# Up product of the second MLP with both halves of the normalised activation in one 512-column operand, from the sixth block on

## The chip, the cores and the metric

One core of a Trainium2 chip runs the whole kernel. The metric is the device time of one execution in microseconds, as the median of several runs; the profile is of one further execution of the same program.

## The reference, cut to what matters

Two decoder layers over 256 tokens of width 1024. Each ends in a gated MLP with a short causal convolution, and the change is in the second of these two MLPs:

```python
def rms_norm(x, gain):
    y = xf * lax.rsqrt(jnp.mean(xf * xf, axis=-1, keepdims=True) + NORM_EPS)
    return (y * gain)

def conv_ffn(x, gain, w_up, conv_w, conv_b, w_down):
    h = rms_norm(x, gain)
    up = causal_dwconv(h @ w_up, conv_w, conv_b)      # 3 taps along the tokens
    g, v = up[..., :D_FF], up[..., D_FF:]             # D_FF = 2816
    return (jax.nn.silu(g) * v) @ w_down
```

All inputs and outputs are float32.

## The kernel before, in words

**Products in three parts.** A float32 product is made of three float32r matmuls: each operand is split into a rounded part (hi) and the rest (lo), and hi·hi, hi·lo and lo·hi are added up in PSUM. `mm3` (L259 to L262) issues the three; L260 and L261 use the weights' hi part with the activation's hi and lo part, L262 the weights' lo part with the activation's hi part. In the up product the weight block is the stationary operand and 256 tokens are the moving columns, so every matmul there has 256 columns and loads its own weights.

**Weights.** `Stream` (L82 to L132) brings every weight tile from HBM over SyncE's queue (L98), and splits it: ScalarE writes the hi part `whi` (L115), VectorE the lo part `wlo` (L119), both of 128x1024. `get` keeps four tiles split ahead; five buffers rotate for each of the two parts, three for the raw tile.

**The MLP** (`ffn`, L508). `split_x` (L341, L342) multiplies x by the norm's gain and splits it; the factor 1/rms per token, `rb`, is not in this operand. The 22 blocks f of 128 hidden channels then follow: 48 matmuls each (2 halves j, gate and value, by 8 chunks k of the width, by 3) into one PSUM bank of 512 columns, gate in the left half and value in the right half (tile `psU`). Banks come from two pools of two, `br` and `bw`, block by block in turn, so four blocks can be in flight. `post` (L524) then takes the bank: L526 multiplies by `rb` from PSUM to SBUF (128x512, VectorE), L531 (ScalarE) and L533 (VectorE) are the convolution, L537 to L539 the gate, L542 and L543 split the result into `ah` and `al`. From the sixth block on (`LAG = 5`), after the up matmuls of block f come the 12 down matmuls of block f-5 (L562; 512 columns each, tile `acc`); after the last block, the down product of the remaining blocks follows.

**Order.** In this part no order is written out by hand. The tile framework plans the order of each engine's queue when the program is built, from its own estimates of durations and from how soon each result is needed; the trace shows the order that it chose. Only in the first layer is a part of the order written by hand. The final norm begins after the last down matmuls.

Of the kernel before, what the change touches and what calls it, by code (L numbers as in the profile page):

```python
# [10 lines left out]
F32 = mybir.dt.float32  # L11
F32R = mybir.dt.float32r
BF16 = mybir.dt.bfloat16
I32 = mybir.dt.int32
AF = mybir.ActivationFunctionType
ALU = mybir.AluOpType
# [3 lines left out]
T = 256  # L20
KT = D // 128
# [5 lines left out]
FT = FF // 128  # L27
# [6 lines left out]
RAW_AHEAD = 2  # L34
SPLIT_AHEAD = 4
LAG = 5
NR = 8


# [100 lines left out]
def _body(ctx, tc, a):  # L140
    nc = tc.nc
    V, S, G, PE, L = nc.vector, nc.scalar, nc.gpsimd, nc.tensor, nc.sync
# [6 lines left out]
    def slots(pool, tag, bufs):  # L149
        return lambda shape, dt=F32, name="t": pool.tile(shape, dt, name=name, tag=tag, bufs=bufs)  # L150

    def banks(pool, tag, bufs):
        return lambda name="ps": pool.tile([128, 512], F32, name=name, tag=tag, bufs=bufs)
# [4 lines left out]
    ba, br, bw = banks(pp, "acc", 4), banks(pp, "r", 2), banks(pp, "w", 2)  # L158
# [25 lines left out]
    def ffn_order(l):  # L184
# [3 lines left out]
        for f in range(FT):  # L188
            o += [up(f), up(FT + f)]
            if LAG <= f < FT - 4 + LAG:  # L190
                o.append(dn(f - LAG))
        o += [dn(f) for f in range(FT - LAG, FT - 4)]
        if l:
# [5 lines left out]
    def by_steps(steps, **lists):  # L199
# [18 lines left out]
    W = Stream(nc, order, rawp, hlp, lambda key: [gains[:, 2 + key[1], 2 * key[2] + i:2 * key[2] + i + 1]  # L218
                                                  for i in range(2)] if key[0] == "mkv" else [None])
# [3 lines left out]
    def views(pool, name, *shapes):  # L223

        n = [int(np.prod(s_)) for s_ in shapes]
        t = pool.tile([128, sum(n)], F32, name=name)
        out = []
        for i, s_ in enumerate(shapes):
            ax = " ".join(f"a{j}" for j in range(len(s_)))
            v = t[:, sum(n[:i]):sum(n[:i + 1])]  # L230
            out.append(v.rearrange(f"p ({ax}) -> p {ax}", **{f"a{j}": d for j, d in enumerate(s_)}))
        return out

    x, gains, ident, s5p, rtok, ones, nhalf, convp, maskf, ropeC, ropeS, rbm, vm1 = views(
        const, "held", (KT, T), (8, KT), (128,), (3, NP), (2,), (1,), (1,), (2, 4, 2 * FT), (128,), (T,), (T,), (T,),
        (2, MEMW))
# [22 lines left out]
    def mm3(out, whi, wlo, ahi, alo, first, last):  # L259
        PE.matmul(out, whi, ahi, start=first, stop=False, skip_group_check=True)  # L260
        PE.matmul(out, whi, alo, start=False, stop=False, skip_group_check=True)  # L261
        PE.matmul(out, wlo, ahi, start=False, stop=last, skip_group_check=True)  # L262
# [8 lines left out]
    def squares(src, ts=None):  # L271
        ts = [] if ts is None else ts
        for s_ in src:
            t = sq([128, 512], name="sq")
            S.activation(t, s_, AF.Square)  # L275
            ts.append(t)
        return ts
# [12 lines left out]
    def root(p):  # L290

        m = sm.tile([128, 2], F32, name="m")
        V.tensor_scalar(m, p[:, :2], 1.0 / D, EPS, op0=ALU.mult, op1=ALU.add)
        return newton(m, 2)
# [21 lines left out]
    def rms(src, bk=bw):  # L316
        y = root(sums(squares(src), bk))
        rb = sm.tile([128, T], F32, name="rb", bufs=2)
        S.activation(rb, spread(y, bk), AF.Copy)
        return rb, y  # L320

    def xbanks():
        return [x[:, 2 * b:2 * b + 2].rearrange("p a t -> p (a t)") for b in range(4)]

    def rb2(rb):
        return rb[:, None, :].to_broadcast([128, 2, T])

    def v2(ap):
        return ap.rearrange("p (a t) -> p a t", t=T)
# [178 lines left out]
    def ffn(l, gi):  # L508
        with tc.tile_pool(name=f"ffn{l}", bufs=1) as pool:
            sl, sa = slots(pool, "s", 12), slots(pool, "a", 2 * LAG + 2)  # L510
            act = split_x(gi)
            rb, _ = rms(xbanks(), bk=bw if l else ba)
            dacc = None
            if l:

                dacc = [ba("acc") for _ in range(4)]
                for k in range(KT):
                    for t in range(2):
                        c = 128 * (k % 4)
                        PE.matmul(dacc[2 * t + k // 4][:, c:c + 128], x[:, k, 128 * t:128 * t + 128], ident,  # L520
                                  start=k % 4 == 0, stop=False, skip_group_check=True)
            acts = {}

            def post(f, p):  # L524
                u = sl([128, 2, T], name="u")
                V.tensor_mul(u, v2(p), rb2(rb))  # L526
                y = sl([128, 2, T], name="y")
                for j in range(2):
                    c = j * FT + f
                    cp = lambda i: convp[:, l, i, c:c + 1]  # L530
                    S.activation(y[:, j], u[:, j], AF.Identity, bias=cp(3), scale=cp(2))  # L531
                    for d in (1, 2):
                        V.scalar_tensor_tensor(y[:, j, d:], u[:, j, :T - d], cp(2 - d), y[:, j, d:],  # L533
                                               op0=ALU.mult, op1=ALU.add)
                g, v = y[:, 0], y[:, 1]
                th = sl([128, T], name="th")
                S.activation(th, g, AF.Tanh, scale=0.5)  # L537
                V.scalar_tensor_tensor(th, th, 1.0, g, op0=ALU.add, op1=ALU.mult)
                V.tensor_mul(th, th, v)  # L539
                ah, al = sa([128, T], F32R, "ah"), sa([128, T], F32R, "al")  # L540
                if l:
                    S.activation(ah, th, AF.Copy, scale=0.5)  # L542
                    V.scalar_tensor_tensor(al, th, 0.5, ah.bitcast(F32), op0=ALU.mult, op1=ALU.subtract)  # L543
                else:
                    S.activation(ah, th, AF.Copy)
                    V.tensor_sub(al, th, ah.bitcast(F32))
                acts[f] = (ah, al)

            def down(f):
                if l:  # L550
                    whi, wlo = W.get(("dn", l, f))
                    for t in range(2):
                        down_tokens(t, (0, 1), f, whi, wlo, False)
                else:
                    gemm(dacc, ("dn", l, f), (f,), acts.get, 0, 8, f == 0, False)

            def down_tokens(t, hs, f, whi, wlo, last):

                ah, al = (p[:, 128 * t:128 * t + 128] for p in acts[f])
                for a_, w_ in ((ah, whi), (ah, wlo), (al, whi)):  # L560
                    for i, h in enumerate(hs):
                        PE.matmul(dacc[2 * t + h], a_, w_[:, 512 * i:512 * i + 512], start=False,  # L562
                                  stop=last and a_ is al, skip_group_check=True)

            for f in range(FT):
                p = (br if f % 2 else bw)("psU")
                w = [None, None]
                todo = [(j, k) for j in range(2) for k in range(KT)]
                for j, k in todo:
                    if w[j] is None:  # L570
                        w[j] = W.get(("up", l, j * FT + f))
                    c = slice(128 * k, 128 * k + 128)
                    mm3(p[:, 256 * j:256 * j + 256], w[j][0][:, c], w[j][1][:, c], *act(k),
                        k == 0 and j == 0, k == KT - 1)
                post(f, p)
                if LAG <= f < FT - 4 + LAG:
                    dacc = dacc or [ba("acc") for _ in range(4)]
                    down(f - LAG)
            for f in range(FT - LAG, FT - 4):
                down(f)  # L580
            if l:
                for h in range(2):
                    for ks in (LAST[:2], LAST[2:]):
                        whi, wlo = W.get(("dnq", l, ks, h))
                        for t in range(2):
                            for i, f in enumerate(ks):
                                c = slice(512 * i, 512 * i + 512)
                                down_tokens(t, (h,), f, whi[:, c], wlo[:, c], f == FT - 1)
                return dacc
            for b in range(4):  # L590
                gemm(dacc, ("dnq", l, b), LAST, acts.get, 2 * b, 2, False, True)
            residual(dacc, 0.5)


    def layer0(pool, s5):
        sr, sh = slots(pool, "r", NR), slots(pool, "h", 4)
        sc = [slots(pool, f"c{i}", 4 - 3 * i) for i in range(2)]
# [617 lines left out]
    with tc.tile_pool(name="fin", bufs=1) as pool:  # L1215
# [4 lines left out]
        for t in range(2):  # L1220
# [7 lines left out]
            for h in range(2):  # L1228
                o = so([128, 512], name="o")
                V.scalar_tensor_tensor(o, accs[2 * t + h], y, gf[h], op0=ALU.mult,  # L1230
                                       op1=ALU.mult)
# [52 lines left out]
```

## Time and profile before

| | |
|---|---|
| median of 3 runs | 671.42 us (670.06 to 672.51) |
| profiled execution | 671.97 us |
| its span, first to last instruction | 670.2 us (1.77 us lie around it) |
| TensorE (PE) busy | 629.2 us, 94% |
| VectorE (DVE) busy | 547.5 us, 82% |
| ScalarE (ACT) busy | 408.0 us, 61% |
| GpSimd (POOL) busy | 103.7 us, 15% |
| second MLP, first up matmul to last down matmul | 472.4 to 662.4 us |

All times of the trace are microseconds from the start of the span. Durations of matmuls overlap (a new one starts every 0.12 or 0.23 us while each takes 0.28 or 0.39 us by the profile), so what one costs is read from the distance of the starts. VectorE's records overlap a little as well: a 128x256 operation of 0.42 us is followed by the next after 0.34 us.

### The profile page before, as it was taken

The numbers are of one execution on the slowest core, as the hardware profiler recorded it, in microseconds if no ns is written. First come the engines' busy times: TensorE is split into PE (matmuls) and PEld (weight loads), VectorE is DVE, ScalarE is ACT, GpSimd is POOL, SyncE is SP. The second block draws the span as 40 slices with busy tenths as digits, with TensorE's granted clock in tenths as the row PEclk, the third lists the DMA queues.
The fourth block names the chain that finished last, engine by engine and source line by source line (L and its number), as shares of the span: only waits on it lengthen the run. The fifth ranks groups of instructions, "written<-read, shape, count | busy, mean of one in ns | idle before, by whom it ended". The sixth has DMA issues, their size and how long they took to land.

```text
span 670.2 us, 12678 instructions
## 1 busy us (share of the span) xinstructions
PE 629.2 (94%) x4968; PEld 595.2 (89%) x4968; DVE 547.5 (82%) x1011; ACT 408.0 (61%) x746; POOL 103.7 (15%) x117
## 2 busy tenths in 40 slices
PE   6787597999999999999999998999999999999995
PEld 5676586899999999999999997879999999999984
DVE  7989899786699988787769799875479998888872
ACT  5597454675566556565548788774446665555641
POOL 4596303031200000000003226301200000000000
PEclk9799698899999999999999997999999999999998
DMA  8722313256457436455465142424345555555511
GB/s 301 253 96 63 104 48 119 95 190 220 155 191 251 169 117 236 157 205 188 149 237 173 65 166 99 150 73 165 109 138 189 193 183 186 186 188 189 189 33 63
DMA packets 43356, 105.24 MB, mean 157 GB/s; under 512 B 3744, under 2 KB 14240, under 8 KB 43296
## 3 DMA queue, kind: packets, MB, share of 16 engines
q1 hardware_dynamic: 42720, 103.84, 45.6%
q8 instruction: 39, 0.64, 0.4%
q10 hardware_dynamic: 576, 0.59, 0.3%
q14 instruction: 21, 0.17, 0.1%
HBM read 103.37 MB, written 1.05 MB: 156 GB/s over the span
## 4 chain that ended last, share of the span: by engine, by line
PE 76%; DVE 18%; ACT 2%; issue 2%; DMA 0%; POOL 0%; DVEq 0%; ACTq 0%
PE psU L262 13%; PE psU L260 12%; PE psU L261 12%; PE acc L562 9%; PE acc L261 7%; PE acc L262 7%; PE acc L260 7%; DVE wlo L119 2%; DVE X L642 1%; PE psO L481 1%; DVE xt L642 1%; PE ps L388 1%; DVE cf L649 1%; DVE Vd L642 1%; PE psT L465 1%
## 5 line engine op out<-in xcount | busy, mean ns | idle before, releaser
L115 ACT ACTIVATE whi<-wraw 128x1024 fp32r<-128x1024 f32 (+1 forms) x176 | 181.1, 1037 | 102.7 <-PE psU L261 52.0
L119 DVE TENSOR_TENSOR wlo<-wraw,whi 128x1024 fp32r<-128x1024 f32 (+1 forms) x176 | 212.8, 1212 | 31.2 <-PE psU L262 14.9
L262 PE MATMUL psU<-xhi,wlo 128*128 128x256 f32 x704 | 197.6, 281 | 1.1 <-DVE wlo L119 1.1
L260 PE MATMUL psU<-xhi,whi 128*128 128x256 f32 x704 | 198.0, 282 | 0.0
L261 PE MATMUL psU<-xlo,whi 128*128 128x256 f32 x704 | 197.4, 281 | 0.0
L262 PEld LDWEIGHTS psU<-xhi,wlo 128*128 128x128 f32 x704 | 133.2, 189 | 1.4 <-DVE wlo L119 1.3
L261 PEld LDWEIGHTS psU<-xlo,whi 128*128 128x128 f32 x704 | 132.6, 189 | 0.7
L260 PEld LDWEIGHTS psU<-xhi,whi 128*128 128x128 f32 x704 | 132.4, 188 | 0.7
L533 DVE SCALAR_TENSOR_TENSOR y<-u,held,y 128x254 f32<-128x254 f32 (+1 forms) x176 | 77.9, 477 | 1.5 <-ACT y L531 1.3
L531 ACT ACTIVATE y<-u,held 128x256 f32<-128x256 f32 x88 | 47.7, 590 | 20.6 <-DVE u L526 20.6
L526 DVE TENSOR_TENSOR u<-psU,rb 128x512 f32<-128x512 f32 x44 | 30.3, 688 | 33.3 <-PE psU L262 33.1
L261 PE MATMUL acc<-al,whi 128*128 128x256 f32 x176 | 49.6, 282 | 0.0
L260 PE MATMUL acc<-ah,whi 128*128 128x256 f32 x176 | 49.6, 282 | 0.0
L262 PE MATMUL acc<-ah,wlo 128*128 128x256 f32 x176 | 49.6, 282 | 0.0
L280 POOL TENSOR_TENSOR sq<-sq 128x512 f32<-128x512 f32 x5 | 8.2, 1648 | 229.7 <-ACT sq L275 229.7
L866 PE MATMUL acc<-xg,wraw 128*128 128x256 f32 x128 | 34.5, 431 | 5.5 <-ACT xg L856 5.5
L866 PEld LDWEIGHTS acc<-xg,wraw 128*128 128x128 f32 x128 | 27.8, 222 | 10.0 <-ACT xg L856 5.5
L262 PEld LDWEIGHTS acc<-ah,wlo 128*128 128x128 f32 x176 | 33.6, 191 | 0.0
L261 PEld LDWEIGHTS acc<-al,whi 128*128 128x128 f32 x176 | 33.6, 191 | 0.0
L260 PEld LDWEIGHTS acc<-ah,whi 128*128 128x128 f32 x176 | 33.5, 190 | 0.0
L262 PE MATMUL acc<-xhi,wlo 128*128 128x256 f32 x112 | 31.6, 283 | 0.0
L261 PE MATMUL acc<-xlo,whi 128*128 128x256 f32 x112 | 31.4, 281 | 0.0
(253 smaller groups left out, 1322.8 us busy)
## 6 DMA issues: line engine op xcount, KB each, us to landing
wraw<-w_up SPq DMA_DIRECT2D x88, 512.0 KB, 4.2
wraw<-w_down SPq DMA_DIRECT2D x44, 512.0 KB, 4.0
wraw<-w_out SPq DMA_DIRECT2D x16, 512.0 KB, 3.6
wraw<-w_in SPq DMA_DIRECT2D x15, 512.0 KB, 5.7
wraw<-w_mem_kv SPq DMA_DIRECT2D x8, 512.0 KB, 3.8
wraw<-w_kv SPq DMA_DIRECT2D x6, 512.0 KB, 7.4
wraw<-w_kv SPq DMA_DIRECT2D x8, 384.0 KB, 3.4
wraw<-w_glu SPq DMA_DIRECT2D x6, 384.0 KB, 3.7
```

Of the source, the lines that this page charges most:

```text
L115: self.nc.scalar.activation(hi[:, c], t[:, c], AF.Copy, scale=1.0 if g_ is None else g_)
L119: self.nc.vector.tensor_sub(lo[:, c], t[:, c], hi[:, c].bitcast(F32))
L260: PE.matmul(out, whi, ahi, start=first, stop=False, skip_group_check=True)
L261: PE.matmul(out, whi, alo, start=False, stop=False, skip_group_check=True)
L262: PE.matmul(out, wlo, ahi, start=False, stop=last, skip_group_check=True)
L280: G.tensor_add(ts[0], ts[0], ts[1])
L526: V.tensor_mul(u, v2(p), rb2(rb))
L531: S.activation(y[:, j], u[:, j], AF.Identity, bias=cp(3), scale=cp(2))
L533: V.scalar_tensor_tensor(y[:, j, d:], u[:, j, :T - d], cp(2 - d), y[:, j, d:], op0=ALU.mult, op1=ALU.add)
L562: PE.matmul(dacc[2 * t + h], a_, w_[:, 512 * i:512 * i + 512], start=False, stop=last and a_ is al, skip_group_check=True)
L642: V.tensor_tensor(o, a_, b_, op=op)
L866: PE.matmul(acc[2 * h + b][:, 256 * (m % 2):256 * (m % 2) + 256], w[:, 512 * i + 128 * m:512 * i + 128 * m + 128], xg[k // 2][:, k % 2], s ...
```

## The change

In the second MLP, from block 5 on (`NORMED = (FT, 5)`: never in the first MLP), the activation operand is the fully normalised x. `normalise(b)`, called in blocks 1 to 4 for two chunks of the width each, multiplies x by gain and by `rb` on VectorE (into `xn`), takes the hi part on ScalarE and the lo part on VectorE, and leaves both side by side in one tile `hl[k]` of 2x256 columns. The up product of these blocks then has two matmuls for each half and chunk: weights' hi part with all 512 columns (hi and lo), and weights' lo part with the 256 hi columns. Each half has a PSUM bank of its own, one of `br` and one of `bw`, with the main sum left and the hi·lo sum right; `post` copies the right half to SBUF on ScalarE and adds the left one to it on VectorE, in place of the product with `rb`. Two new tags take SBUF: 8 tiles `n` and 2 tiles `g` of 2 KB a partition.

```diff
+NORMED = (FT, 5)
...
+            sn, sg, hl = slots(pool, "n", KT * l), slots(pool, "g", 2 * l), []
...
+            def normalise(b):
+
+                t = sg([128, 2, T], name="xn")
+                for i in range(2):
+                    k = 2 * b + i
+                    V.scalar_tensor_tensor(t[:, i], x[:, k], gains[:, gi, k:k + 1], rb, op0=ALU.mult, op1=ALU.mult)
+                for i in range(2):
+                    n = sn([128, 2, T], F32R, "xhl")
+                    S.activation(n[:, 0], t[:, i], AF.Copy)
+                    V.tensor_sub(n[:, 1], t[:, i], n[:, 0].bitcast(F32))
+                    hl.append(n)
+
             def post(f, p):
                 u = sl([128, 2, T], name="u")
-                V.tensor_mul(u, v2(p), rb2(rb))
+                if f < NORMED[l]:
+                    V.tensor_mul(u, v2(p), rb2(rb))
+                else:
+                    for j in range(2):
+                        S.activation(u[:, j], p[j][:, T:], AF.Copy)
+                        V.tensor_add(u[:, j], p[j][:, :T], u[:, j])
...
             for f in range(FT):
-                p = (br if f % 2 else bw)("psU")
-                w = [None, None]
-                todo = [(j, k) for j in range(2) for k in range(KT)]
-                for j, k in todo:
-                    if w[j] is None:
-                        w[j] = W.get(("up", l, j * FT + f))
-                    c = slice(128 * k, 128 * k + 128)
-                    mm3(p[:, 256 * j:256 * j + 256], w[j][0][:, c], w[j][1][:, c], *act(k),
-                        k == 0 and j == 0, k == KT - 1)
+                p = (br if f % 2 else bw)("psU") if f < NORMED[l] else [b_("psU") for b_ in (br, bw)]
+                for j in range(2):
+                    whi, wlo = W.get(("up", l, j * FT + f))
+                    for k in range(KT):
+                        c = slice(128 * k, 128 * k + 128)
+                        if f < NORMED[l]:
+                            mm3(p[:, 256 * j:256 * j + 256], whi[:, c], wlo[:, c], *act(k), k == 0 and j == 0, k == KT - 1)
+                        else:
+                            PE.matmul(p[j], whi[:, c], hl[k].rearrange("p a t -> p (a t)"), start=k == 0, stop=False,
+                                      skip_group_check=True)
+                            PE.matmul(p[j][:, :T], wlo[:, c], hl[k][:, 0], start=False, stop=k == KT - 1,
+                                      skip_group_check=True)
+                if l and 0 < f <= 4:
+                    normalise(f - 1)
                 post(f, p)
```

## Rows read from the trace of the kernel before

**Rows 1.** The page: busy time by engine, and the clock in 40 slices.

```profile
PE 629.2 (94%) x4968; PEld 595.2 (89%) x4968; DVE 547.5 (82%) x1011; ACT 408.0 (61%) x746; POOL 103.7 (15%) x117
...
PEclk9799698899999999999999997999999999999998
```

**Rows 2.** The chain that ended last, from 470 us on, by line.

```profile
by line: PE acc L562 29.7%; PE psU L262 20.9%; PE psU L260 20.9%; PE psU L261 20.7%; PE acc L520 1.8%; DVE o L1230 0.8%; DVE wlo L119 0.6%; issue 0.5%; PE ps L286 0.4%; ACT sq L1223 0.3%; DVEq L1280 0.3%; POOL y L299 0.3%; PE ps L312 0.2%; 
```

**Rows 3.** Busy time in three stretches: PE, PEld, DVE, ACT, POOL, clock, DMA, GB/s.

```profile
485.31:490.69 5.38, 5.38 (x48) 5.38 (x47) 1.23 (x2) 1.08 (x2) 0.00 (x0) 1.00 0.45 157
490.69:513.15 22.46, 22.46 (x181) 21.92 (x179) 21.77 (x38) 14.90 (x24) 0.00 (x0) 1.00 0.48 161
513.15:646.22 133.07, 133.07 (x950) 125.07 (x948) 113.59 (x186) 79.37 (x117) 0.00 (x0) 1.00 0.55 178
```

**Rows 4.** TensorE in order of time, blocks 5 to 21: start, duration, instruction.

```profile
510.35 0.63 PE L562 MATMUL acc<-whi,ah 128*128 128x512 f32 x2
...
513.15 0.28 PE L260 MATMUL psU<-xhi,whi 128*128 128x256 f32 x1
...
515.97 0.28 PE L260 MATMUL psU<-xhi,whi 128*128 128x256 f32 x1
...
518.84 0.63 PE L562 MATMUL acc<-whi,ah 128*128 128x512 f32 x2
...
527.30 0.62 PE L562 MATMUL acc<-whi,ah 128*128 128x512 f32 x2
...
530.09 0.28 PE L260 MATMUL psU<-xhi,whi 128*128 128x256 f32 x1
...
646.22 0.62 PE L562 MATMUL acc<-whi,ah 128*128 128x512 f32 x2
```

**Rows 5.** TensorE in order of time, last 48 down matmuls: first and last.

```profile
651.77 0.39 PE L562 MATMUL acc<-whi,ah 128*128 128x512 f32 x1
...
662.42 0.39 PE L562 MATMUL acc<-whi,al 128*128 128x512 f32 x1
```

**Rows 6.** Groups by line and shape, from 450 us: busy us, mean ns.

```profile
L526 DVE TENSOR_TENSOR u<-psU,rb 128x512 f32<-128x512 f32 x22 | 15.1, 688 | 15.0 <-PE psU L262 15.0
L539 DVE TENSOR_TENSOR th<-th,y 128x256 f32<-128x256 f32 x22 | 9.3, 421 | 0.4
L543 DVE SCALAR_TENSOR_TENSOR al<-th,ah 128x256 fp32r<-128x256 f32 x22 | 9.2, 420 | 1.8 <-ACT ah L542 1.5
L542 ACT ACTIVATE ah<-th 128x256 fp32r<-128x256 f32 x22 | 9.0, 408 | 4.1 <-DVE th L539 4.1
L342 DVE SCALAR_TENSOR_TENSOR xlo<-held,xhi 128x256 fp32r<-128x256 f32 x8 | 4.5, 606 | 0.0
L504 DVE TENSOR_TENSOR olo<-psO,ohi 128x256 fp32r<-128x256 f32 x2 | 0.8, 424 | 5.0 <-ACT ohi L503 5.0
L319 ACT ACTIVATE rb<-ps 128x256 f32<-128x256 f32 x1 | 0.4, 385 | 9.1 <-PE ps L312 9.1
```

**Rows 7.** VectorE in order of time: the bank evacuations, and the last block's end.

```profile
490.69 0.69 DVE L526 TENSOR_TENSOR u<-psU,rb 128x512 f32<-128x512 f32 x1 [1.66 <-PE psU L262]
...
517.94 0.68 DVE L526 TENSOR_TENSOR u<-psU,rb 128x512 f32<-128x512 f32 x1
518.54 0.41 DVE L543 SCALAR_TENSOR_TENSOR al<-th,ah 128x256 fp32r<-128x256 f32 x1
...
544.50 0.69 DVE L526 TENSOR_TENSOR u<-psU,rb 128x512 f32<-128x512 f32 x1 [0.54 <-PE psU L262]
...
652.47 0.43 DVE L543 SCALAR_TENSOR_TENSOR al<-th,ah 128x256 fp32r<-128x256 f32 x1 [0.48 <-ACT ah L542]
```

**Rows 8.** Waits from 490 to 655 us: us in total, times, longest.

```profile
ACT whi L115 <- PE psU L261: 30.7, 27, 2.4
...
DVE wlo L119 <- PE psU L262: 2.3, 4, 1.0
```

**Rows 9.** TensorE in order of time: its one wait in the second MLP.

```profile
481.54 0.39 PE L262 MATMUL psU<-xhi,wlo 128*128 128x256 f32 x1 [1.14 <-DVE wlo L119]
```

## The prediction

> **What bounds the kernel now.** The page comes first: TensorE is busy for 94% of the span and its clock is full nearly everywhere [rows 1]. Next is the chain that ended last, from 470 us on, because the change lies there: 62.5% of it are the three up matmuls and 29.7% the down matmuls [rows 2], so the second MLP ends when TensorE has worked through its stream. The table by stretches says how near the others are. From 485 to 646 us TensorE is busy without a gap at clock 1.00. VectorE has 4.15 us free of 5.38 just after the norm's factor is there, then almost nothing (21.77 busy of 22.46 us, blocks 2 to 5), then some room (113.59 of 133.07 us); ScalarE has room all along and GpSimd does nothing [rows 3]. So a microsecond less on TensorE is a microsecond less of time, as long as VectorE, the tight one in blocks 0 to 5, does not come to stand in its way.
>
> **What it removes on TensorE.** Blocks 5 to 21 are 17 blocks of 16 pairs (half, chunk), 272 pairs. In each, two 256-column matmuls on the same weights become one of 512 columns; the third one stays. What one costs is the distance of the starts. From the first down matmul of block 5 (510.35) to that of block 21 (646.22) are 16 blocks in 135.87 us, 8.492 us a block; 12 of its matmuls are down matmuls of 512 columns, which took 2.79 us in the block shown (527.30 to 530.09), 0.2325 us each [rows 4]. The 48 up matmuls thus take 8.492 - 2.79 = 5.70 us, 0.1188 us each. A second price of 512 columns is in the tail: 48 matmuls from 651.77 to 662.42, 47 distances, 0.2266 us each [rows 5]. The new matmul is like the tail's in that it stays in one bank and loads new weights each time, and like the down matmuls inside the blocks in that weights are being split and loaded beside it. So one pair saves 2 x 0.1188 - 0.2325 = 0.0051 us or 2 x 0.1188 - 0.2266 = 0.0110 us, and all 272 save 1.4 or 3.0 us. It resembles both, so I take the middle, **2.2 us**, and keep both ends. Seen so, the change is small because a 256-column matmul already costs little more than half of a 512-column one.
>
> The Trainium skill has a rule that speaks against even this: in "TensorE: Matmul & The Clock Gate", section "Back-to-back issue gap", an isolated warm matmul of N columns costs N/2.4 ns and about 2.5 ns more. By that the merging would save 2.5 ns a pair, an estimated 0.7 us in all. The rows differ from it: at 2.4 GHz 256 columns are 106.7 ns, and the 118.8 ns measured leave 12 ns beside them. The sum goes by the rows.
>
> **What it adds ahead of block 5.** `normalise` runs four times with 4 VectorE operations of 128x256 and 2 ScalarE copies. Scalar-tensor-tensor and tensor-tensor of this shape take 0.42 us in this stage, by L543 and L539 [rows 6], and one can follow the other after 0.34 us (the next operation after al at 518.54 started 0.33 us later). So 16 operations are 16 x 0.34 = 5.4 us of VectorE; from above, by L342, the same kind of operation while x was split at 0.606 us [rows 6], it would be 16 x 0.606 = 9.7 us. I take 5.4: the slow rows of L342 lie in a stretch in which GpSimd worked, and here it does nothing [rows 3]. ScalarE adds 8 x 0.41 = 3.3 us, by L542. What covers them: `rb` is there at 485.31, and until 490.69 VectorE has 4.15 us free [rows 3]. The planner puts ready work into idle slots, so most of the work should go there, limited by the two `xn` buffers. Left over are about 1.3 us in the full stretch behind it. They push back the posts, which have room: `al` of block 3 comes at 518.54 [rows 7], while its down product runs in block 8, from 535.84 on (518.84 plus two blocks of 8.49). If the cover is gone, all 5.4 us push. The splits of weights stay ahead, too: where ScalarE waits for something in this stage, it is mostly for TensorE to give a buffer back (27 times, 30.7 us) [rows 8], thus it runs as far ahead as the buffers let it. SyncE's loads follow the lo splits, which free the raw buffers; they shift with VectorE by the same 1 to 2 us, in a queue that is nowhere late for TensorE. I cost this part at 0.
>
> **What it changes in `post`.** For 17 blocks one VectorE operation of 128x512 from PSUM (0.688 us, L526) becomes two of 128x256 (0.424 us each, L504), 0.16 us more by busy time and 2 x 0.34 - 0.61 = 0.07 us more by distance; ScalarE gets two copies of 128x256 from PSUM, 2 x 0.385 us by L319 [rows 6]. VectorE is at 85% and ScalarE at 60% in these blocks [rows 3], so both fit: 0 on the path. Each ScalarE copy waits for its half's last matmul, and queued behind it are splits of the next weights, which have four tiles, two blocks, in hand. At the end, block 21's `al` comes at 652.47 + 0.43 = 652.90 [rows 7]; its down product is the 16th of the last 48 matmuls, so it starts at 651.77 + 15 x 0.2266 = 655.17. One copy more in this chain is 0.4 us, and the 2.2 us of room covers it.
>
> **Banks.** Each block now takes two of the four banks, so a block's bank must be read before the block after the next begins, not four blocks later. Block 5 is read at 517.94, until 518.62 [rows 7]. Block 7 would start at 518.84 + 2.79 = 521.6, so VectorE may fall 3.0 us further behind than now before TensorE waits. The 1.3 us left over keep inside that. By block 9, at 544.50, VectorE waits for TensorE again [rows 7], so the lag is worked off. Cost 0.
>
> **The sum.** 671.97 us for the profiled execution (span 670.2 and 1.77 around it) less 2.2 is 669.8. That execution stands 0.55 us above the median of 671.42, to which the forecast is given: **669.2 us**, and 668.4 to 670.0 by the two ends.
>
> **The rivals.**
> - *The merging buys nearly nothing* (0.20). If the new matmul costs 0.2325 and the ones merged are of the fast kind, 24 of them from 513.15 to 515.97 at 0.1175 us [rows 4], a pair saves 0.0025 us, 0.7 us in all: 670.7. For it: the 512-column matmuls next to splits and loads were at 0.2325. Against it: they go to two banks in turn, and the average up matmul is at 0.1188.
> - *Slower: the last normalised chunk is late* (0.15). Block 5 needs all eight `hl` tiles in its first eight pairs, at 510.35 - 5.70 = 504.65. VectorE is full before that, and the order is the planner's. If it puts the normalising behind the posts of the early blocks, TensorE stands still at block 5. From the point where the last `hl` comes after 504.65, every microsecond counts in full; beyond 2.2 us the change is a loss. For it: the full 22.46 us stretch. Against it: the idle 4.15 us ahead of it, and lo splits that the planner already places between the pieces of a post. Price: the whole work unhidden, 5.4 us, gives 669.2 + 5.4 = 674.6.
> - *Better on both counts* (0.15). The new matmul at the tail's 0.2266, and with the planner's new order the one wait of 1.14 us in this MLP [rows 9] gone: 671.42 - 3.0 - 1.1 = 667.3. That wait is ahead of the changed blocks, so nothing makes it go but a different order.
>
> The forecast keeps 0.50.
>
> **The numbers.** A measurement of this kernel can tell about 0.3%, 2.0 us, from no change, so the border is 669.4. The forecast's own range, savings from 1.4 to 3.0 us, lies for about 0.6 beyond 2.0: 0.30 faster and 0.20 same. With the better case 0.45 are faster. Same is 0.20 + 0.20 and 0.02 of the late case (a short wait), 0.42; slower is the remaining 0.13. The range runs from 666.9, just below the better case, to 672.1, which takes in the case without gain and a wait of up to 2.9 us on top of the forecast; the full late case is left out.
>
> **What would show it.** Right: in blocks 5 to 21 pairs of starts (512 then 256 columns) 0.345 to 0.351 us apart in place of three at 0.356; blocks 8.492 - 0.13 = 8.36 us long; no TensorE idle before block 5 or block 7; normalising on VectorE between 485.3 and 504.6, much of it before 490.7; the evacuation of block 5 no later than 521.6. Wrong: a wait of TensorE for `xhl` or for a bank, a clock below 1.00 behind such a wait, blocks that do not get shorter, or time that changes ahead of 485 us because the planner ordered other parts anew.

## The result, and where the time went

The changed kernel takes **675.73 us** (median of 5 runs) against 671.42 us: a ratio of 1.0067, 95% interval 1.0045 to 1.0090, so **slower by about 4.3 us**, outside the range. In a second series, of 12 runs, it took 673.78 us, ratio 1.0038 [1.0020 to 1.0055]. One thing has to be known to read such numbers: repeated executions of the kernel before lie in two groups, near 669.8 and near 672.0 us, so a microsecond between two medians is not read as an effect, and the argument below goes by ratios with their intervals and by stages of the trace.

The profiled execution after took 675.73 us, span 673.9. The page's lines that answer to [rows 1]:

```profile
PE 627.5 (93%) x4696; PEld 581.4 (86%) x4696; DVE 555.2 (82%) x1044; ACT 420.0 (62%) x788; POOL 100.9 (15%) x117
...
PEclk9898699799999999999999998899999999999998
```

272 matmuls fewer, VectorE and ScalarE with the work that was added, and the span is nevertheless 3.7 us longer. The same matmul can be found in both traces by its number, since TensorE's order is the same up to the second MLP. The distances between five such matmuls make a table of stages (us, each worked out from two starts; the first MLP is counted up to one of its last down matmuls, at 347.18 before, and the last column is a start):

| profiled execution | to the first MLP | first MLP | from there to the second MLP | its blocks 0 to 4 | its blocks 5 to 21 | last matmul |
|---|---|---|---|---|---|---|
| before | 165.51 | 181.67 | 125.22 | 32.22 | 157.82 | 662.42 |
| after | 168.86 | 182.54 | 126.73 | 32.34 | 155.73 | 666.21 |
| difference | +3.35 | +0.87 | +1.51 | +0.12 | -2.09 | +3.79 |

The part that was changed became 2.09 us shorter. **The loss, 5.7 us, lies in three stages whose code and order of matmuls are untouched.**

First the changed part. Groups by line and shape after 490 us (busy us, mean ns; the last part is idle time before them and who ended it):

```profile
L594 PE MATMUL psU<-xhl,whi 128*128 128x512 f32 x272 | 95.9, 394 | 0.0
L596 PE MATMUL psU<-xhl,wlo 128*128 128x256 f32 x272 | 76.2, 280 | 0.0
...
L546 DVE TENSOR_TENSOR u<-psU,u 128x256 f32<-128x256 f32 x34 | 13.8, 419 | 9.3 <-ACT u L545 9.3
...
L545 ACT ACTIVATE u<-psU 128x256 f32<-128x256 f32 x34 | 12.3, 376 | 11.0 <-PE psU L596 10.9
```

The new matmuls have 0.0 us of idle time ahead of them: TensorE never waits for a normalised tile or for a bank. TensorE in order of time, the first pairs of block 5's second half and the first down matmuls of blocks 20 and 21:

```profile
515.81 0.39 PE L594 MATMUL psU<-xhl,whi 128*128 128x512 f32 x1
516.04 0.28 PE L596 MATMUL psU<-xhl,wlo 128*128 128x256 f32 x1
516.16 0.39 PE L594 MATMUL psU<-xhl,whi 128*128 128x512 f32 x1
...
641.60 0.63 PE L582 MATMUL acc<-whi,ah 128*128 128x512 f32 x2
...
649.94 0.63 PE L582 MATMUL acc<-whi,ah 128*128 128x512 f32 x2
```

A pair takes 516.16 - 515.81 = 0.35 us; over all, the 512-column matmul is followed after 0.2325 us and the 256-column one after 0.1173 us, 0.3498 together, where three took 0.3566. A block takes 649.94 - 641.60 = 8.34 us in place of 8.49. The table by stretches (as [rows 3]) has TensorE without a gap, and VectorE fuller than before but not full:

```profile
490.00:496.00 6.00, 6.00 (x53) 6.00 (x52) 4.87 (x11) 2.96 (x6) 0.00 (x0) 1.00 0.01 3
496.00:515.00 19.00, 19.00 (x147) 18.35 (x146) 17.98 (x33) 12.53 (x20) 0.00 (x0) 1.00 0.79 288
515.00:650.00 135.00, 135.00 (x715) 115.49 (x714) 120.15 (x218) 92.60 (x158) 0.00 (x0) 1.00 0.47 163
```

Now the stage in which most was lost. From the waits between 30 and 44 us (engine, line, who ended it: us in total, times, longest), the kernel before:

```profile
POOL ee L639 <- DVE E L642: 2.0, 1, 2.0
DVE uT L874 <- ACT rb L1015: 0.8, 1, 0.8
```

and after:

```profile
DVE uT L899 <- ACT rb L1040: 3.2, 1, 3.2
ACT rb L1040 <- POOL E L664: 2.4, 1, 2.4
POOL ee L664 <- DVE E L667: 2.0, 1, 2.0
```

A wait is there that was not there before: ScalarE's copy of the first layer's norm factor `rb` (L1015, now L1040) waits 2.4 us for GpSimd's operations on `E`, with which it has nothing to do, and VectorE's first use of `rb` waits with it. The reason is in the memory maps of the two built programs, the lists of each tile's address in SBUF. SBUF is packed up to the same highest address in both (229,344 bytes per partition), and the framework finds each tile's address by itself. The change adds twelve tiles of 2 KB, up to ten of them alive at a time. Of the 973 tiles that both programs have under one name, 867 lie elsewhere after it, most of them in code that was not touched:

```
            rb of layer 0         scratch tiles `et` at that address before it
before      222368 .. 223392      none
after       202528 .. 203552      four (202528 .. 203872)
```

The first three of these `et` are written and read by VectorE, the last one by GpSimd. In the new map `rb` takes over memory that GpSimd is still using, so its writer must wait for GpSimd: in the built program the copy waits for a GpSimd operation, where before it waited for a matmul.

### The profile page after: what moved, and what is told of

The parts are those of the page before. It is cut to its first block, busy times and chain, and to the rows that moved or that the text cites. A ratio compares the mean times of both kernels' runs of the same rounds, so it can differ in the third digit from the quotient of the medians.

```text
span 673.9 us, 12184 instructions
## 1 busy us (share of the span) xinstructions
PE 627.5 (93%) x4696; PEld 581.4 (86%) x4696; DVE 555.2 (82%) x1044; ACT 420.0 (62%) x788; POOL 100.9 (15%) x117
## 4 chain that ended last, share of the span: by engine, by line
PE 75%; DVE 18%; ACT 2%; issue 2%; POOL 1%; DMA 1%; DVEq 0%; ACTq 0%
PE psU L594 9%; PE acc L582 9%; PE psU L264 8%; PE psU L262 8%; PE psU L263 8%; PE acc L263 7%; PE acc L264 7%; PE acc L262 7%; PE psU L596 5%; DVE wlo L121 2%; DVE X L667 1%; DVE xt L667 1%; PE psO L483 1%; PE ps L390 1%; ACT P L453 1%
## 5 line engine op out<-in xcount | busy, mean ns | idle before, releaser
L264 PE MATMUL psU<-xhi,wlo 128*128 128x256 f32 x432 | 121.9, 283 | 1.1 <-DVE wlo L121 1.1
L262 PE MATMUL psU<-xhi,whi 128*128 128x256 f32 x432 | 121.7, 283 | 0.0
L263 PE MATMUL psU<-xlo,whi 128*128 128x256 f32 x432 | 121.3, 282 | 0.0
L594 PE MATMUL psU<-xhl,whi 128*128 128x512 f32 x272 | 95.9, 394 | 0.0
L264 PEld LDWEIGHTS psU<-xhi,wlo 128*128 128x128 f32 x432 | 82.1, 190 | 1.5 <-DVE wlo L121 1.3
L553 DVE SCALAR_TENSOR_TENSOR y<-u,held,y 128x255 f32<-128x255 f32 (+1 forms) x176 | 79.5, 477 | 3.2 <-ACT y L551 2.9
L263 PEld LDWEIGHTS psU<-xlo,whi 128*128 128x128 f32 x432 | 82.1, 190 | 0.0
L596 PE MATMUL psU<-xhl,wlo 128*128 128x256 f32 x272 | 76.2, 280 | 0.0
L594 PEld LDWEIGHTS psU<-xhl,whi 128*128 128x128 f32 x272 | 51.0, 188 | 11.8
L596 PEld LDWEIGHTS psU<-xhl,wlo 128*128 128x128 f32 x272 | 51.3, 189 | 0.7
```

The costliest lines, as they stand in the source:

```text
L594: PE.matmul(p[j], whi[:, c], hl[k].rearrange("p a t -> p (a t)"), start=k == 0, stop=False, skip_group_check=True)
L596: PE.matmul(p[j][:, :T], wlo[:, c], hl[k][:, 0], start=False, stop=k == KT - 1, skip_group_check=True)
```

## The experiments

**Theory 1**: the new tiles make the framework pack SBUF anew; by that `rb` gets its wait, and other stages get longer, while the merging gains about what was forecast. **Rival 2**: the added work in the second MLP costs. **Rival 3**: all of the loss comes from the one wait. **Rival 4**: not the wait, but the order of the first loads costs; the plan had moved the load of the constants `s5c` behind three others (it does so in every kernel whose `rb` waits, unless forced).

All profiled executions by stage; the kernels are described one by one below the table. In the rows above *before* `rb` waits for GpSimd, in *before* and the rows under it it does not:

| profiled execution | to the first MLP | first MLP | between | blocks 0 to 4 | blocks 5 to 21 | time, ratio to before |
|---|---|---|---|---|---|---|
| after (twice) | 168.86, 167.28 | 182.54, 182.54 | 126.73, 126.37 | 32.34, 32.35 | 155.73, 155.73 | 1.0067, 1.0038 |
| after, loads as before | 165.82 | 182.51 | 126.39 | 33.85 | 155.73 | 1.0049 |
| before, wait added | 165.54 | 181.53 | 125.24 | 33.70 | 157.82 | 1.0033 |
| the same, loads as before | 165.60 | 181.60 | 124.05 | 31.46 | 157.82 | 0.9986 |
| by chunk, wait added | 166.81 | 181.54 | 125.15 | 31.46 | 156.10 | 0.9983 |
| the same, loads as before | 168.18 | 181.55 | 125.11 | 31.46 | 156.10 | 0.9984 |
| *before* | 165.51 | 181.67 | 125.22 | 32.22 | 157.82 | 1 |
| before, `rb` apart | 163.89 | 181.67 | 125.18 | 33.66 | 157.82 | 0.9989 |
| after, `rb` apart | 164.77 | 182.54 | 126.39 | 33.85 | 155.72 | 1.0018 |
| before, tiles held | 163.39 | 183.88 | 125.66 | 31.63 | 157.95 | 1.0039 |
| after, by chunk | 164.24 | 181.54 | 125.14 | 31.45 | 156.10 | 0.9954 |
| after, one `xn` | 163.33 | 181.61 | 125.61 | 31.50 | 155.96 | 0.9961 |
| normalised, not merged | 164.22 | 181.65 | 125.15 | 31.47 | 157.53 | 0.9979 |

**The wait alone, in the kernel before.**

```diff
...
+                if (i, r) == (0, 3):
+                    tc.add_manual_dep(d["rb"], pool_ops[-1].name, mybir.DependencyInfo(
+                        mybir.DependencyClass.Sync, mybir.DependencyReason.DATA), reason="wait")
...
```

> The kernel before, no tile moved, with one dependency added: ScalarE's copy of the first layer's rb also waits for the last GpSimd operation of the layer's powers, as it does after the change (there because rb lies on an address that these operations still use). Theory 1 (placement makes this wait): rb about 36.6 us in place of 33.7 us and about 3.5 us on the whole time, so about 674.9 us; the first MLP's matmul spacing stays at 118.3 ns, since no weight tile moved. Rival 2 (what the added work in the second MLP costs): no change, 671.4 us. Rival 3 (the wait also brings the slower spacing of the first MLP and the longer attention): 671.4 + 5.7 = 677.1 us.

673.48 us, ratio 1.0033 [1.0017 to 1.0050]: 2.2 us lost. With no tile moved, the first MLP (181.53) and the stage behind it (125.24) stayed as before, so rival 3 falls: the wait does not bring the other two losses. It does cost, but less than the 3.5 us expected. The table's first stage does not show this cost (165.54 against 165.51), and what the profiled execution took longer lies in blocks 0 to 4. The matmuls that the kernel before starts from 82 to 116 us come 2.7 to 2.8 us later with the wait, those from 123 us on no later: in between, TensorE's clock was low for longer in the kernel before. TensorE from 120 to 122 us (busy time, granted clock, share and rate of the DMAs), before and with the wait:

```profile
120.00:122.00 2.00, 2.00 (x6) 0.50 0.00 0
120.00:122.00 2.00, 2.00 (x16) 1.00 0.00 0
```

So the cost of the wait is read from the times of many executions, and the single trace shows only that it reached TensorE.

**`rb` in a place of its own**, in the changed kernel and in the kernel before.

```diff
-        rb = sm.tile([128, T], F32, name="rb", bufs=2)
+        rb = const.tile([128, T], F32, name="rb0")
```

> The changed kernel with the first layer's rb in a place of its own, so that its copy waits for no GpSimd work; 6 tiles move. Theory 1: 3 to 3.5 us less than the changed kernel, 672.2 to 672.7 us, with rb at 33.7 us; the first MLP's spacing stays at 119.2 ns, as its weights lie where the changed kernel has them. Rival 2 (the added work costs): no change, 675.7 us. Rival 3 (the wait brings all of the 5.7 us): 670 us.

> The kernel before with the same edit (rb of the first layer in a place of its own; 17 tiles move). There rb waited for nothing, so theory 1 and both rivals: 671.4 us, within 0.7 us.

The changed kernel without the wait: 671.98 us, 1.0018 [1.0004 to 1.0032]; before with the same edit: 670.46 us, 0.9989 [0.9971 to 1.0006]. So the edit gives 1.3 us (against 1.0038) to 3.3 us (against 1.0067) where there was a wait, and nothing that can be told where there was none. The first MLP stayed at 182.54 us, with 6 tiles moved: its loss does not come from the wait. Rival 2 does not explain a gain by an edit in the first layer.

**The memory alone, without the work.** The same twelve tiles are only held in the second MLP, by small GpSimd writes; all products are as before.

```diff
...
+            def hold(b):
+
+                t = sg([128, 2, T], name="xn")
+                G.memset(t[:, :, :1], 0.0)
+                for i in range(2):
+                    n = sn([128, 2, T], name="xhl")
+                    G.tensor_copy(n[:, :, :1], t[:, :, :1])
...
```

> The kernel before with the change's ten new tiles held in SBUF through the second MLP (small GpSimd writes and copies), without the normalising and with the up products as before. 856 of 959 tiles move; rb does not wait here. Theory 1 (placement alone shifts the time, with no added work): ahead of the second MLP other times than before, by 0 to 2.5 us, from the spacing of the first MLP's matmuls and the waits of the attention, so 671.4 to 673.9 us. Rival 2 (the added work costs): 671.4 us, and the trace as before up to the second MLP.

672.75 us, 1.0039 [1.0023 to 1.0055]: by the ratio 2.6 us slower, a little over the expected 0 to 2.5, while the median lies inside the expected 671.4 to 673.9. Nothing of the change's work on TensorE, VectorE or ScalarE is in it, and the first MLP is 183.88 us long, 2.2 us more than before. Holding up to 20 KB costs this kernel time in a stage in which those tiles do not exist. In the profiled execution the first stage was 2.1 us shorter and hid that.

**The same change, packed otherwise.** Two harmless variants of `normalise`: chunk by chunk with four half-sized `xn` tiles, and as in the change but with one `xn` tile.

```diff
-            sn, sg, hl = slots(pool, "n", KT * l), slots(pool, "g", 2 * l), []
+            sn, sg, hl = slots(pool, "n", KT * l), slots(pool, "g", 4 * l), []
...
-                t = sg([128, 2, T], name="xn")
                 for i in range(2):
                     k = 2 * b + i
...
+                    t = sg([128, T], name="xn")
...
```

> The changed kernel, but the normalising goes chunk by chunk (four xn tiles of half the size in place of two): the same sums, another lifetime of the small tiles, so another packing. In it the first layer's rb waits for no GpSimd work, and 7 of the 8 tiles of the split x in the first MLP lie where the kernel before has them. Theory 1 (placement lost the time, the merging gains): first MLP at a spacing of 118.2 to 118.7 ns, the second MLP 1.9 us shorter than before, so 669.5 us in all (668.5 to 670.5). Rival 2 (the added work in the second MLP costs): 675.7 us as the changed kernel.

> The changed kernel with one xn tile in place of two. Less cover for the normalising (each pair waits until the one before is read), and again another packing: rb waits for no GpSimd work, and the split x of the first MLP lies partly where it did. Theory 1: 669.5 to 671 us. Rival 2 (the added work costs): 675.7 us or more, since the normalising has less room.

By chunk: **667.91 us, 0.9954 [0.9938 to 0.9969]**; one `xn`: 668.30 us, 0.9961 [0.9947 to 0.9975]. Both are faster than either kernel, by about 3 us against before, although the arithmetic is that of the change and the second has less room for its normalising. Rival 2 is out. Against the changed kernel they win in every stage ahead of block 5; in blocks 5 to 21 they are 0.2 to 0.4 us longer. They gain 0.8 us on the kernel before in blocks 0 to 4 as well: the one wait of TensorE there, 1.14 us in [rows 9] and 1.1 in the changed kernel, is down to 0.3 us, as the waits of TensorE by chunk, from 466 to 490 us, have it:

```profile
PE psU L264 <- DVE wlo L121: 0.3, 1, 0.3
```

**The work without the merging.** The tiles are normalised and held to the end, but every block multiplies as before.

```diff
-NORMED = (FT, 5)
+NORMED = (FT, FT)
...
+                if l and f == FT - 1:
+                    for n in hl:
+                        G.tensor_copy(n[:, 0, 1:2], n[:, 0, :1])
```

> The changed kernel without the merging: the eight normalised tiles are made and held to the last block (small GpSimd writes), but every block multiplies as the kernel before. In this packing rb waits for nothing, and the split x of the first MLP lies exactly as in the kernel before. Theory 1: nothing to gain and nothing lost, 671.4 us, the second MLP as long as before within 0.3 us, since the normalising is hidden. Rival 2 (the added work costs): 4 us or more above before. If the normalising hides only in part, the second MLP is longer by up to 5.4 us.

669.30 us, 0.9979 [0.9966 to 0.9992], 1.4 us faster than before by the new packing. Set beside the version by chunk, the first four stages agree within 0.11 us (164.22 and 164.24, 181.65 and 181.54, 125.15 and 125.14, 31.47 and 31.45), so this is the cleanest comparison of the study. Blocks 0 to 4, which hold all of the normalising, take 31.47 us, and 31.46 in the version "before, wait added, loads as before", which has none of it: it is hidden. Blocks 5 to 21 take 157.53 without and 156.10 with the merging: **the merging by itself is worth 1.43 us** between these two, 2.09 us between the kernels before and after. Of the 3 us that the version by chunk gains on the kernel before, about half came with the new packing and not with the change.

**The order of the loads.** Rival 4 was open, because every kernel with the wait also had `s5c` late. Forced back to the order of before, first in the kernel before with the wait:

```diff
...
+        for late, early in ((dM, dC), (dW, dM), (dB, dW)):
+            tc.add_manual_dep(getattr(late, "ins", late), getattr(early, "ins", early).name, mybir.DependencyInfo(
+                mybir.DependencyClass.NoSync, mybir.DependencyReason.DATA), reason="order")
```

> The kernel before with the added wait of rb, and with the constants' loads kept in the kernel before's order (s5c first; it comes one load of x earlier than there), where the plan with the wait had put s5c last. Theory 1 (the wait itself costs): 2 to 3 us above before, rb at 36 us or later. Rival 4 (the late load of s5c costs, not the wait): as before, 671.4 us.

669.97 us, 0.9986 [0.9972 to 1.0000]: as rival 4 had it, not theory 1. But the edit had moved most tiles too (1,132 of 1,258), and the table shows the time won elsewhere: 1.2 us between the MLPs and 0.8 in blocks 0 to 4 against before, and nothing in the first stage (165.60 and 165.54). It settles nothing, so the question was put again where hardly a tile moves: in the changed kernel (3 tiles) and in the version by chunk (none), the changed kernel beside them once more.

> The changed kernel once more, unaltered, on the chip of the three kernels below, so that they have it beside them. 675.5 us, within 1 us.

> The changed kernel with the constants' loads held to the kernel before's order (s5c early); rb still waits for GpSimd and only 3 tiles move. Theory 1 (the wait costs): 675 to 676 us, as the changed kernel. Rival 4 (the late load of s5c costs): about 3 us less, 672 to 673 us, as the kernel with rb in a place of its own, which also had s5c early.

> The chunk-by-chunk version (667.9 us, rb waits for nothing) with one dependency added: rb's copy waits for the last GpSimd operation of the layer's powers. No tile moves; the plan puts s5c last again. Theory 1 and rival 4 both: 2 to 3.5 us more, 670 to 671.4 us, with the whole difference made by 115 us. If neither the wait nor the order of loads costs: 667.9 us.

> The same as the kernel just ahead (rb waits, no tile moves), with the constants' loads in the kernel before's order (s5c early). Theory 1 (the wait costs): 670 to 671.4 us, as with s5c late. Rival 4 (the late load costs): 667.9 us, as the chunk-by-chunk version.

The changed kernel took 673.78 us, 1.0038 [1.0020 to 1.0055], lower than expected; with the loads in the old order 673.84 us, 1.0049 [1.0032 to 1.0065]. By chunk with the wait added: 670.15 us, 0.9983 [0.9970 to 0.9997]; with the old order 670.35 us, 0.9984 [0.9968 to 1.0000], against 0.9954 without the wait. Two pairs, and the order of the loads changes neither: rival 4 falls. With no tile moved, and each ratio taken to the kernel before on the same chip, the wait is worth 0.0029 to 0.0030, 2.0 us, with some 1.4 us either way by the two intervals together. The waits from 30 to 44 us by chunk,

```profile
ACT Bz L791 <- DVE X L666: 3.2, 2, 2.2
...
DVE uT L898 <- ACT rb L1039: 0.8, 1, 0.8
```

and by chunk with the wait added:

```profile
DVE uT L904 <- ACT rb L1045: 3.2, 1, 3.2
ACT rb L1045 <- POOL E L665: 2.4, 1, 2.4
```

show the same two lines that tell before from after.

**What the three losses come to.** The wait: 1.3 to 3.3 us by the pairs above, 2.0 and 2.2 where no tile moved; over all profiled executions the first stage takes 166.9 us on average with it (7, from 165.5 to 168.9) and 164.2 without (7, from 163.3 to 165.5). The first MLP: 0.87 us, in each of the four profiled executions with the changed kernel's map (182.51 to 182.54); the other maps but one have 181.53 to 181.67. The stage between: 1.15 to 1.5 us, in the same four; its waits of TensorE (392 to 430 us) after

```profile
PE psT L467 <- DVE P L460: 2.0, 1, 2.0
PE psS L434 <- DVE ks L425: 1.9, 1, 1.9
PE acc L264 <- DVE wlo L121: 0.6, 1, 0.6
```

and before

```profile
PE psT L465 <- DVE P L458: 2.1, 1, 2.1
PE psS L432 <- DVE ks L423: 1.0, 1, 1.0
```

have 0.9 and 0.6 us more. That these come from reused addresses as the first one does is argued, not shown: no experiment took them away one by one. With the wait at 2.0 to 2.7 us, 0.1 for blocks 0 to 4 and -2.1 for the merging, the sum is 2.0 to 3.1 us. By their ratios the two series gave 2.5 and 4.5; the first stage of the same program differed by 1.6 us between their profiled executions (168.86 and 167.28).

## Why the prediction was wrong

- **The saving on TensorE: right.** Forecast 2.2 us (1.4 to 3.0), measured 2.09 in blocks 5 to 21, and 1.43, the lower end, in the cleanest comparison. That the middle was met between before and after is luck: the new matmul takes 0.2325 us, as the down matmuls inside the blocks [rows 4] and not the middle to the tail's 0.2266 [rows 5], which by itself is the lower end, 1.4 us; the 256-column matmul behind it takes 0.1173 in place of 0.1188, 0.4 us more, and the down matmuls inside the blocks, which the forecast left as they were, became 0.3 us shorter together. The pair's 0.3498 lies inside the 0.345 to 0.351 announced, the block's 8.34 at the 8.36. The rule of the Trainium skill weighed there ("TensorE: Matmul & The Clock Gate", section "Back-to-back issue gap"), which is for an isolated matmul, would have a pair save an estimated 2.5 ns; the trace disagrees with it here, 356.6 - 349.8 = 6.8 ns.
- **The normalising hidden: right.** VectorE in order of time, its first and its last operation:

```profile
491.07 1.68 DVE L532 SCALAR_TENSOR_TENSOR xn<-held,rb 128x256 f32<-128x256 f32 x4 [2.24 <-ACT rb L321]
...
502.21 0.42 DVE L536 TENSOR_TENSOR xhl<-xn,xhl 128x256 fp32r<-128x256 f32 x1
```

  The last tile is there at 502.63, and block 5's first matmul comes at 510.48. It went less into the idle time and more between other work than forecast, which cost nothing, as the kernel without the merging shows. The 0.606 us of L342 that the forecast set aside is the mean of one operation of 1.52 us and seven of 0.47 to 0.48; the normalising's own products with gain and `rb` took 0.48.
- **`post`: right.** 0.419 us twice on VectorE (forecast 0.424) and 0.376 us twice on ScalarE (0.385); VectorE is at 120.15 of 135 us.
- **Banks: right, but not for the reason given.** ScalarE begins to read block 5's banks at 528.26. By the forecast's rule they had to be read by 521.6, shifted by 5.9 us 527.5. TensorE does not wait, since the plan put down matmuls between the halves of blocks 5 and 6, so that block 7 begins at 532.76.
- **The late chunk: did not happen**, although its price, 674.6 us, is near the result. A fitting total is no evidence for a mechanism. The other two rivals did not come either: the pair saves more than 2.5 ns, and the new matmul is at 0.2325 with the wait of [rows 9] still there.
- **The step that failed is the sum.** "671.97 us for the profiled execution [...] less 2.2 is 669.8" holds everything outside the second MLP at what it was. That had no line, no bound and no rival of its own; all three rivals lay at or behind the second MLP. The text named "time that changes ahead of 485 us because the planner ordered other parts anew" as a sign of being wrong, and that came, by way of placement more than of order. In place of nothing, the runs show 5.7 us there (3.35, 0.87 and 1.51 us by stage). The new tiles were looked at for their buffers' order (two `xn`) and never for the memory they take from a full SBUF. What such a repacking can do is now known for this kernel: ahead of the second MLP, 470.6 to 478.1 us in the executions profiled, a range wider than the gain that was forecast, of which about 2 us lie between the two executions of the changed kernel alone (478.1 and 476.2).

## What to carry to other kernels

Where a framework packs SBUF by itself and SBUF is full, new tiles in one stage can bring waits and another matmul spacing into stages that nobody touched: compare the traces stage by stage first, and look for waits between instructions that share no data. Judge a change of one or two microseconds in more than one packing (a tile more or less, another size) before it is kept or thrown away; here the same change was 2.5 to 4.5 us slower in one packing and 3 us faster in another. And where the memory is full, a forecast needs a range for repacking, from both sides.

## What the runs showed of the hardware that was not expected

**Matmul spacing goes with the placement.** In the first MLP, where the code, the order and the clock (1.00) are the same in all versions, the mean distance of up matmuls (without the two to four above 140 ns) was 118.28 ns before, 118.28 with the wait added (no tile moved), 118.28 with `rb` apart, 119.09 in the changed kernel and again 119.09 with `rb` apart, and 119.97 with the tiles only held. The parts of the split x lie from 38,976 to 160,928 bytes in the first three, all but two of eight tiles above 208,000 in the next two, and all above 183,000 in the last. Inside the changed kernel the matmuls on its two low tiles follow after 118.7 and 117.1 ns, those on the others after 118.7 to 119.8. With one `xn`, though, one of the eight lies at 226,464, and the mean is 118.28. That the moving operand's address is the cause was not tried by itself, and the weights' tiles lie elsewhere in the slower maps too.

**TensorE's clock can fall after a short wait, or not.** Behind the wait of 1.14 us at 481.5, the kernel before (the columns are TensorE's busy time, granted clock, share and rate of the DMAs):

```profile
480.00:482.00 2.00, 0.86 (x7) 1.00 0.00 0
482.00:484.00 2.00, 2.00 (x19) 1.00 0.00 0
```

and the same code with the added wait far ahead of it:

```profile
480.00:482.00 2.00, 0.86 (x5) 0.86 0.00 0
482.00:484.00 2.00, 2.00 (x12) 0.50 0.02 6
```

12 matmuls in place of 19 in 2 us, at 1.2 in place of 2.4 GHz. The stage differs by 1.5 us, 32.22 and 33.70 in the table. It came in four of the seven profiled executions that had the long wait, and in none of the seven that had it at 0.3 us or so. So this wait could cost more than its own length. In the first stage the clock falls in other places from one execution to the next. The kernel before, TensorE at the end of the first layer's mixing:

```profile
112.00:116.00 4.00, 2.55 (x12) 0.59 0.87 321
116.00:120.00 4.00, 3.33 (x15) 0.50 0.06 21
120.00:124.00 4.00, 4.00 (x13) 0.63 0.09 24
```

and the kernel before with the tiles held, in which the matmuls from 82 to 113 us were 0.4 us behind and those from 126 us on 2.5 us ahead:

```profile
112.00:116.00 4.00, 1.66 (x12) 1.00 0.06 11
116.00:120.00 4.00, 2.57 (x18) 1.00 0.93 334
120.00:124.00 4.00, 4.00 (x28) 1.00 0.37 114
```

A drop of this kind is as large as the wait that was to be priced in that stage, which is why single traces did not agree on it and times of many executions were needed.
